# Small products wait for company before they enter the stream of projections

## The chip, the cores and the metric

The kernel runs on one core of one Trainium2 chip. The metric is the device time of one execution in microseconds (us). Three executions took 1216.67, 1216.26 and 1215.63 us (median 1216.26); the execution that was profiled took 1215.75 us.

## The reference

Three transformer-like layers are applied to 256 tokens of width 1024, all in fp32. Layers 0 and 1 have the same form (`hybrid_layer`): a projection `h @ w_in` makes the inputs of three branches, a native sparse attention (NSA, 8 heads of 64), a gated linear attention (GLA, 4 heads) and a cross-attention into 256 memory tokens (4 heads of 128). Their outputs are multiplied with branch weights, gated and summed, projected by `w_out`, added to x, and then an MLP of width 4096 with a squared ReLU follows. Layer 2 (`hybrid_layer_2`) has a spatial gating branch, a depthwise convolution of 31 taps with a layer norm, and an attention of 8 heads of 64 (MoBA), merged in the same way. Cut to the frame:

```python
x = first_block(x, mem, ...)      # DEPTH = 2 times hybrid_layer
return second_block(x, ...)       # once hybrid_layer_2
# hybrid_layer: z = rms_norm(x) @ w_in; o_nsa, o_gla, o_mem from parts of z
merged = gates0 * (o_nsa @ w_branch[0]) + gates1 * (o_gla @ w_branch[1]) + gates2 * (o_mem @ w_branch[2])
x = x + merged @ w_out
return x + jnp.square(jax.nn.relu(rms_norm(x) @ w_up)) @ w_down
```

## The kernel before

Every large fp32 product is made of three fp32r products: activations and weights are each split into a rounded high part and the rest (`hi` and `lo`, tiles `hx`, `oh`, `ol`, `b8x`). Weights come in units of 128 x 1024 by DMA (`raw`); ScalarE or GpSimd makes `hi` (L441, L439), VectorE makes `lo` (L442). These large products write the four PSUM banks `acc` and are called the stream here. 512-column products of the stream follow one another every 0.227 us, 256-column ones every 0.12 us.

Everything else on TensorE is small: transposes against the identity (L192), attention scores, the GLA levels, the sums over heads. These are written as Python generators, called chains. A chain emits a few products and the work on the other engines that depends on them, then yields a number: how many nanoseconds later, by the order's own clock, its next step shall come. The small products use three PSUM banks `psm` and one, `pso`, for sums over several steps.

The order of TensorE's instructions is written out by hand, in the order in which Python emits them (`manual_schedule` for PE alone, L119 and around); the other engines' orders are found by the framework. The order's clock is a number that each emitted product advances by an estimate (`pe_time` L175: 217.6 for a 512-column fp32r product, 108.8 for a 256-column one, n x 1.69 but at least 214 for an fp32 product, 107 for a transpose). The rules:

- `start` (L143) puts a chain on the list `chains` with a due time. `advance` (L130) runs one step of it and sets the next due time to the clock plus the yielded number; an ended chain leaves the list.
- `pump` (L138) is called from inside the stream and advances every chain that is due. `tok_major` (L493) calls it after three 512-column products, `transposed` (L507) after six 256-column ones: every 652.8 of the clock either way. `up_first` (L1365) calls it after two products, `dn` after three.
- `finish(c)` (L148) advances chains in the order of their due times, moving the clock ahead where needed, until `c` has ended. `need(hh, k)` (L157) does the same until the part k of a transposed activation has been emitted.

The chains that matter here. In layers 0 and 1: `mem_chain` (L639), `nsa_qk` (L699), `nsa_cmp` (L758), `nsa_att` (L882) and `gla` (L991) are alive together while the projections of gates and values stream. `nsa_att` yields 350 again and again until q and k are there and the memory attention has ended. The stream calls `finish` for the memory chain, `gla` and `nsa_att` (L1302 to L1308) before the branch product that reads each. At a layer's end `x_transposed` (L539) transposes the new x in four steps of four transposes: for the last two it yields 2750 until `halves` says that the second half of x is there, then 1000 (`XLAT`), then a step, 300, and the last step. Its result `hx` is needed by `up_first`, whose second half begins with part 4. In layer 0 alone a further chain, the transposition of the memory for layer 1, is started 7000 ahead of its first step before `up_first` (L1402).

In layer 2: `conv` (L1468) has 30 steps of VectorE work with 5000 between them, then a product with ones for the mean (four products of 256 columns), 4450 later one for the variance, and then the norm. `moba` (L1521) is started 1000 ahead, when 48 pumps have passed since `conv` began. It has twelve steps with products: scores (1729 of the clock), 6500 later the next scores, 6500 later transposes (642), 2000 later the sums (1298), 3000 later scores, and so on. 80 pumps later the stream reaches `finish(c_att)` (L1617), after 16 products `psm<-a,n` without a pump. From there the stream has 128 pumps (gates and branch product of branches 2 and 0, gates of branch 1) to `finish(c_conv)` (L1632), behind which the norm's result is split into `oh`, `ol` and multiplied with the branch weights. When `moba` has ended, `conv` is the only chain on the list.

Of the kernel before, what the change touches and what calls it, by code (L numbers as in the profile page):

```python
# [29 lines left out]
WARM2 = 4  # L30
NRAW = 4
XLAT = 1000.0
CO_IDENT = 0
CO_HM = 128
CO_CM = CO_HM + 8
# [11 lines left out]
def shape_constants():  # L47
    p = np.arange(128)
    cf = np.zeros((128, CO_END), np.float32)
    cf[:, CO_IDENT:CO_IDENT + 128] = np.eye(128)  # L50
    ml = np.zeros((9, 128, 128), np.float32)
# [47 lines left out]
def block_kernel(ctx, tc, x_in, mem_in, positions, ln_mix, w_in, b_merge, nsa_q_norm, nsa_k_norm,  # L99
# [27 lines left out]
    clock = [0.0]  # L127
    chains = []

    def advance(c):  # L130
        lat = next(c[0], None)
        if lat is None:
            c[2] = True
            chains.remove(c)
        else:
            c[1] = clock[0] + LATF * lat

    def pump():  # L138
        for c in list(chains):
            while not c[2] and c[1] <= clock[0]:  # L140
                advance(c)
# [94 lines left out]
    def PS():  # L236
        return psm.tile([P, 512], F32, tag="psm", name=nm("psm"))
# [59 lines left out]

    IDF = CF[:, CO_IDENT:CO_IDENT + 128]
    IDB = CBT[:, CB_IDENT:CB_IDENT + 128]
# [193 lines left out]
    def tok_major(hh, hl, w2d, r0, nk, cols, fine=False, paired=None):  # L493
        n = sum(c1 - c0 for c0, c1 in cols)
        ps = [ACC(), ACC()]
        ws = units(w2d, r0, nk, cols, paired, fine)
        for k, (wh, wl) in enumerate(ws):
            need(hh, k)
            if fine and k == 0:
                warm(WARM2)  # L500
            for tt in range(2):
                ts_ = slice(tt * P, tt * P + P)
                mm3(ps[tt][:, :n], hh[:, k, ts_], hl[:, k, ts_], wh, wl, k == 0, k == nk - 1)
                pump()
        return ps

    def transposed(hh, hl, w2d, r0, nk, c0, ps, paired=None):  # L507
        ws = units(w2d, r0, nk, [(c0, c0 + 256)], paired)
        for cb in range(2):
            o = ps[:, cb * 256:cb * 256 + 256]  # L510
            for k, (wh, wl) in enumerate(ws):
                cs = slice(cb * P, cb * P + P)
                mm(o, wh[:, cs], hh[:, k, :], k == 0, False)
                mm(o, wh[:, cs], hl[:, k, :], False, False)
                mm(o, wl[:, cs], hh[:, k, :], False, k == nk - 1)
                if k % 2 == 1:
                    pump()
        return ps
# [20 lines left out]
    def x_transposed(src, hh, hl, gcol, prog, halves):  # L539
        for k in range(0, 8, 2):  # L540
            if halves is not None:
                if halves[0] <= k // 4:
                    while halves[0] <= k // 4:
                        yield 2750.0
                    yield XLAT
            pt = PS()
# [665 lines left out]
    def layer(l, hT):  # L1212
# [116 lines left out]
        def up(gi):  # L1329
            uh, ul = OT()  # L1330
            p2 = up_first() if gi == 0 else None
            for c in range(2):
                r = T2("gtmp")
                ws = units(w_up[l], 0, 8, [(gi * 512 + c * 256, gi * 512 + c * 256 + 256)]) if gi else None
                for cb in range(2):
                    rs = r[:, 256 * cb:256 * cb + 256]
                    if gi == 0:
                        ps = p2[2 * c + cb]
                    else:
                        ps = PS()  # L1340
                        for part in range(2):
                            for k in range(8):
                                up_product(ps, k, cb, ws[k][part], part)
                            pump()
                    act(rs, ps[:, 256:512], AF.Copy)
                    dve.tensor_tensor(rs, ps[:, 0:256], rs, op=OP.add)
                act(r, r, AF.Relu)  # L1347
                uhf = uh[:, 2 * c:2 * c + 2].rearrange("p a b -> p (a b)")
                ulf = ul[:, 2 * c:2 * c + 2].rearrange("p a b -> p (a b)")
                act(uhf, r, AF.Square)  # L1350
                u = T2("tmp")
                pool.tensor_tensor(u, r, r, op=OP.mult)  # L1352
                dve.tensor_tensor(ulf, u, f32(uhf), op=OP.subtract)
            ub[gi] = (uh, ul)
# [365 lines left out]
```

## Time and profile before

| what | value |
|---|---|
| median of three executions | 1216.26 us |
| profiled execution, and its span | 1215.75 us, 1214.0 us |
| TensorE products (PE) | 1195.1 us busy, 98% of the span, 6553 instructions |
| VectorE (DVE), ScalarE (ACT), GpSimd (POOL) | 72%, 50%, 17% busy |
| HBM read | 211.86 MB, 175 GB/s over the span |

The span is the time between the first and the last instruction. PE rows are products, DVE, ACT and POOL rows are those engines; a row gives its start in us from the span's start, its length, the engine, the line of the code, what it writes and reads, the shape and how many like it follow directly. An [idle before <- what] at the end tells how long the engine had been idle and what it waited for. Products are pipelined and their ends are modelled, so the distance from start to start tells more than a length.

### The profile page before, as it was taken

Reading aid. Unit: us, or ns where it says so; the run is one execution under the profiler, and the core shown is the slowest. Engines: PE = TensorE matmul, PEld = TensorE weight load, DVE = VectorE, ACT = ScalarE, POOL = GpSimd, SP = SyncE. Lnnn points to the kernel's source line nnn. Section 1 sums busy time; section 2 is a strip of 40 time slices with the busy share of each in tenths; the row PEclk is TensorE's granted clock in tenths of the full one; section 3 lists DMA queues with packets and bytes.
Section 4 is the critical chain, followed back from the end, with each engine's and each line's share of the span. In section 5 each row is a group of like instructions: output and inputs, shape, how many; then the busy total and the mean of one; then the engine's idle time right before and its main releaser. Section 6 shows DMA issues by size and latency. Waiting matters only on the chain. (4 is left out here: it accounts for less than half of the span.)

```text
span 1214.0 us, 17754 instructions
## 1 busy us (share of the span) xinstructions
PE 1195.1 (98%) x6553; PEld 1001.3 (82%) x6553; DVE 869.8 (72%) x1457; ACT 605.0 (50%) x988; POOL 202.1 (17%) x235
## 2 busy tenths in 40 slices
PE   8999999999999999999999999999999999999997
PEld 6897777888888888888777888888888998998886
DVE  5967878667755556658878867665555699995587
ACT  7567544434645545466645444464454344453351
POOL 2310320120111112200222020121121111010201
PEclk9999999999999999999999999999999999999999
DMA  8567533677566666657723576656566655557652
GB/s 278 182 179 198 156 97 112 191 214 214 166 188 189 192 191 190 181 157 187 199 65 105 176 197 195 187 175 196 185 192 198 195 170 162 153 158 212 186 195 87
DMA packets 138699, 213.91 MB, mean 176 GB/s; under 512 B 12145, under 2 KB 76757, under 8 KB 138612
## 3 DMA queue, kind: packets, MB, share of 16 engines
q1 hardware_dynamic: 137284, 209.19, 57.9%
q0 software_dynamic: 1152, 3.31, 0.9%
q8 instruction: 51, 0.84, 0.3%
q14 instruction: 36, 0.29, 0.1%
q10 hardware_dynamic: 176, 0.27, 0.1%
HBM read 211.86 MB, written 1.05 MB: 175 GB/s over the span
## 5 line engine op out<-in xcount | busy, mean ns | idle before, releaser
L442 DVE TENSOR_TENSOR lo<-raw,hi 128x1024 fp32r<-128x1024 f32 (+1 forms) x369 | 458.1, 1245 | 218.5 <-ACT hi L441 163.0
L441 ACT ACTIVATE hi<-raw 128x1024 fp32r<-128x1024 f32 (+1 forms) x308 | 322.6, 1057 | 331.2 <-PE acc L188 267.5
L188 PE MATMUL acc<-hi,hx 128*128 128x512 f32 (+1 forms) x1024 | 337.6, 394 | 0.0
L188 PEld LDWEIGHTS acc<-hi,hx 128*128 128x128 f32 x1024 | 191.3, 188 | 40.0 <-issue 4.0
L188 PE MATMUL acc<-lo,hx 128*128 128x512 f32 (+1 forms) x512 | 196.9, 385 | 0.1
L439 POOL TENSOR_SCALAR hi<-raw 128x1024 fp32r<-128x1024 f32 x61 | 75.5, 1238 | 601.3 <-PE acc L188 424.4
L188 PE MATMUL acc<-hi,oh 128*128 128x512 f32 x400 | 157.9, 395 | 0.0
L188 PE MATMUL acc<-hi,ol 128*128 128x512 f32 x400 | 155.9, 390 | 0.0
L188 PE MATMUL acc<-lo,oh 128*128 128x512 f32 x400 | 155.9, 390 | 0.0
L188 PE MATMUL acc<-hx,hi 128*128 128x256 f32 (+1 forms) x704 | 136.6, 297 | 0.9 <-DVE hx L532 0.7
L188 PEld LDWEIGHTS acc<-hx,hi 128*128 128x128 f32 x704 | 111.0, 191 | 6.0 <-issue 2.3
L188 PE MATMUL psm<-hx,hi 128*128 128x512 f32 x448 | 111.8, 391 | 0.0
L188 PEld LDWEIGHTS acc<-lo,hx 128*128 128x128 f32 x512 | 96.5, 189 | 16.7 <-DVE lo L442 0.6
L188 PE MATMUL acc<-hi,b8x 128*128 128x512 f32 (+1 forms) x336 | 105.0, 385 | 0.0
L188 PE MATMUL acc<-hx,lo 128*128 128x256 f32 x384 | 99.7, 283 | 0.0
L188 PEld LDWEIGHTS psm<-hx,hi 128*128 128x128 f32 x448 | 81.4, 189 | 15.1
L188 PEld LDWEIGHTS acc<-hi,ol 128*128 128x128 f32 x400 | 75.1, 188 | 16.2 <-DVE ol L532 0.3
L188 PEld LDWEIGHTS acc<-hi,oh 128*128 128x128 f32 x400 | 75.2, 188 | 14.6
L188 PEld LDWEIGHTS acc<-lo,oh 128*128 128x128 f32 x400 | 75.2, 188 | 14.5
L188 PEld LDWEIGHTS acc<-hi,b8x 128*128 128x128 f32 x336 | 62.2, 188 | 11.7 <-ACT b8x L531 0.2
L188 PEld LDWEIGHTS acc<-hx,lo 128*128 128x128 f32 x384 | 69.9, 191 | 0.6
L1352 POOL TENSOR_TENSOR tmp<-gtmp 128x512 f32<-128x512 f32 x32 | 40.1, 1253 | 166.9 <-ACT gtmp L1347 166.9
(359 smaller groups left out, 1456.9 us busy)
## 6 DMA issues: line engine op xcount, KB each, us to landing
raw<-in_w_in SPq DMA_DIRECT2D x160, 512.0 KB
raw<-in_w_up SPq DMA_DIRECT2D x64, 512.0 KB
raw<-in_w_down SPq DMA_DIRECT2D x64, 512.0 KB
raw<-in_w_branch SPq DMA_DIRECT2D x28, 512.0 KB
raw<-in_w_out SPq DMA_DIRECT2D x24, 512.0 KB
raw<-in_cmp_w SPq DMA_DIRECT2D x32, 256.0 KB
raw<-in_mem_w_kv SPq DMA_DIRECT2D x15, 512.0 KB
raw<-in_w_branch SPq DMA_DIRECT2D x16, 256.0 KB
```

What stands on the lines that cost most here:

```text
L188: nc.tensor.matmul(o, l, r, start=start, stop=stop, skip_group_check=True)
L439: pool.tensor_scalar(hi, raw, 1.0, 1.0, op0=OP.mult, op1=OP.mult)
L441: act(hi, raw, AF.Copy)
L442: dve.tensor_tensor(lo, raw, f32(hi), op=OP.subtract)
L1352: pool.tensor_tensor(u, r, r, op=OP.mult)
```

## The change

`pump` first collects the chains that are due. If there is exactly one, more than one chain is on the list, and the one is less than 800 late on the order's clock, nothing is advanced at this pump. Otherwise all due chains are advanced as before. `finish` and `need` are unchanged.

```diff
+COMPANY = 800
     def pump():
+        due = [c for c in chains if c[1] <= clock[0]]
+        if len(due) == 1 and len(chains) > 1 and clock[0] - due[0][1] < COMPANY:
+            return
         for c in list(chains):
             while not c[2] and c[1] <= clock[0]:
                 advance(c)
```

## Rows read from the trace of the kernel before

**Rows 1.** The page: busy time of each engine, and the chain that ended last by engine.
```profile
PE 1195.1 (98%) x6553; PEld 1001.3 (82%) x6553; DVE 869.8 (72%) x1457; ACT 605.0 (50%) x988; POOL 202.1 (17%) x235
...
PE 33%; DVE 1%; ACT 1%; POOL 0%; issue 0%; DVEq 0%; POOLq 0%; ACTq 0%
```

**Rows 2.** Busy time by stretch (us, then PE, PEld, DVE, ACT, POOL with their counts, granted clock, DMA share, GB/s): the chains of layer 0 after the polling, the stretch behind it, and the chains of layer 1.
```profile
114.00:212.00 98.00, 95.35 (x574) 73.33 (x573) 82.75 (x203) 53.27 (x128) 20.38 (x29) 1.00 0.42 125
212.00:300.00 88.00, 88.00 (x405) 73.01 (x404) 60.39 (x64) 37.43 (x44) 13.50 (x11) 1.00 0.70 205
...
582.00:684.00 102.00, 98.51 (x584) 75.69 (x583) 85.42 (x205) 53.76 (x129) 22.08 (x29) 0.98 0.42 123
```

**Rows 3.** Timeline of PE in these stretches: the longest waits of small products.
```profile
140.11 0.68 PE L188 MATMUL psm<-QB,b8x 128*128 128x128 f32 x4 [0.76 <-DVE tmp L798]
...
149.44 0.55 PE L192 MATMUL psm<-CF,pexp 128*128 128x128 f32 x3 [0.86 <-DVE a L1061]
...
620.69 0.21 PE L192 MATMUL psm<-CF,ck 32*128 32x32 f32 x1 [0.83 <-DVE ck L834]
...
647.39 0.68 PE L188 MATMUL psm<-QB,b8x 128*128 128x128 f32 x4 [1.26 <-DVE a L1061]
```

**Rows 4.** Busy time by stretch in layer 1, right behind 32 products of 16 columns; the column after POOL is the granted clock.
```profile
628.00:631.00 3.00, 3.00 (x14) 1.56 (x13) 2.59 (x12) 0.90 (x2) 0.00 (x0) 0.64 0.00 0
631.00:634.00 3.00, 3.00 (x12) 2.41 (x11) 1.32 (x6) 1.55 (x2) 1.01 (x2) 0.80 0.00 0
```

**Rows 5.** Timeline of PE: four transposes alone in the stream (the product before them, they, and the second product after them).
```profile
273.52 0.39 PE L188 MATMUL acc<-hi,ol 128*128 128x512 f32 x1
273.75 0.60 PE L192 MATMUL psm<-CF,M 128*128 128x128 f32 x4
...
274.42 0.40 PE L188 MATMUL acc<-lo,oh 128*128 128x512 f32 x1
```

**Rows 6.** Timeline of PE, the stream's last product before an entry and its second after it: eight products of `nsa_cmp` alone; a step of `nsa_att` with these eight and four of `gla`; the same step with `gla` alone.
```profile
125.33 0.39 PE L188 MATMUL acc<-hi,hx 128*128 128x512 f32 x1
...
126.56 0.39 PE L188 MATMUL acc<-lo,hx 128*128 128x512 f32 x1
...
130.91 0.40 PE L188 MATMUL acc<-hi,hx 128*128 128x512 f32 x1
...
134.92 0.39 PE L188 MATMUL acc<-lo,hx 128*128 128x512 f32 x1
...
182.04 0.40 PE L188 MATMUL acc<-hi,hx 128*128 128x512 f32 x1
...
185.29 0.39 PE L188 MATMUL acc<-lo,hx 128*128 128x512 f32 x1
```

**Rows 7.** Timeline of PE in layer 0: the last transposes of `gla`, and the first product that reads its result.
```profile
211.64 1.04 PE L192 MATMUL psm<-CF,g 128*128 128x128 f32 x8
...
232.95 0.39 PE L188 MATMUL acc<-hi,oh 128*128 128x512 f32 x1
```

**Rows 8.** Timeline of PE in layer 0, `up_first`: products of the first half's second column block, the last two steps of `x_transposed` (`psm<-CF,X`), the second half's first products, its last part.
```profile
303.80 1.09 PE L188 MATMUL acc<-hx,hi 128*128 128x512 f32 x4
304.73 0.60 PE L192 MATMUL psm<-CF,X 128*128 128x128 f32 x4
...
305.62 0.60 PE L192 MATMUL psm<-CF,X 128*128 128x128 f32 x4
...
307.47 1.56 PE L188 MATMUL acc<-hx,hi 128*128 128x512 f32 x6
...
309.59 0.74 PE L188 MATMUL acc<-hx,hi 128*128 128x512 f32 x2
```

**Rows 9.** Timeline of DVE at the same place (the low parts of `hx`, parts 4, then 5 and 6), and of PE at the like place of layer 1.
```profile
305.87 0.48 DVE L532 SCALAR_TENSOR_TENSOR hx<-psm,COL,hx 128x256 fp32r<-128x256 f32 x1 [0.46 <-ACT hx L531]
306.77 0.88 DVE L532 SCALAR_TENSOR_TENSOR hx<-psm,COL,hx 128x256 fp32r<-128x256 f32 x2 [0.41 <-ACT hx L531]
...
780.40 0.73 PE L188 MATMUL acc<-hx,hi 128*128 128x512 f32 x2 [0.74 <-DVE hx L532]
```

**Rows 10.** Timeline of PE in layer 2: scores of `moba` (first and second), its last transposes, and the 16 products ahead of `finish(c_att)`.
```profile
1011.73 0.93 PE L188 MATMUL psm<-g,g 64*128 64x128 f32 x8
...
1019.85 0.93 PE L188 MATMUL psm<-g,g 64*128 64x128 f32 x8
...
1072.98 0.82 PE L192 MATMUL psm<-CF,pexp 128*128 128x128 f32 x6
...
1078.92 1.95 PE L188 MATMUL psm<-a,n 128*128 128x128 f32 x16
```

**Rows 11.** Timeline of ACT: the two copies that follow the transposes at 1072.98.
```profile
1073.57 0.88 ACT L1556 ACTIVATE pts<-psm 128x384 f32<-128x384 f32 x2 [0.89 <-PE psm L192]
```

**Rows 12.** Timeline of PE: the products of `conv` for the mean and for the variance, and the third product of the branch that reads its result.
```profile
1144.00 1.89 PE L188 MATMUL psm<-b8x,cw 128*128 128x256 f32 x8
...
1150.52 1.89 PE L188 MATMUL psm<-b8x,cw 128*128 128x256 f32 x8
...
1172.23 0.50 PE L188 MATMUL acc<-hi,ol 128*128 128x512 f32 x1
```

**Rows 13.** Timeline of DVE: the first instruction of the norm, and the low part of the branch input at its end.
```profile
1153.78 0.42 DVE L1487 TENSOR_SCALAR a<-psm 128x256 f32<-128x256 f32 x1
...
1170.96 1.21 DVE L532 SCALAR_TENSOR_TENSOR ol<-b8x,oh 128x1024 fp32r<-128x1024 f32 x1
```

## The prediction, made before the change was run

> **What bounds the kernel now.** I read the page first: TensorE (PE) is busy 98% of the span, and the chain that ended last is PE too, the other engines having 1% each or less [rows 1]. So the time is the sum of PE's products plus the places where PE waits, and a change of the order pays or costs only there. Next the busy times by stretch: PE idles 98.00 - 95.35 = 2.65 us while the chains of layer 0 run, 102.00 - 98.51 = 3.49 us in layer 1, and nothing in the 88 us behind them [rows 2]. Together 6.1 us. The timeline of PE shows who waits: small products that come before their input (made by VectorE or GpSimd) or their bank is free, 0.76, 0.86, 0.83 and 1.26 us for the longest [rows 3]. Behind one long run of tiny products in layer 1 the granted clock is 0.64 and 0.80 over two stretches of 3 us [rows 4]: PE fell to 1.2 GHz for 3 x 0.36/0.5 + 3 x 0.20/0.5 = 3.4 us, which is 1.7 us of lost work. Last I read the places where the stream waits for a chain: the end of a layer [rows 8, 9] and layer 2 [rows 10 to 13].
>
> **Part 1: what an entry costs.** From the last stream product before four transposes to the second after them is 274.42 - 273.52 = 0.90 us; two distances of the stream are 0.45, so the four cost 0.45, and 4 x 0.109 (the distance inside a longer run) is 0.44 [rows 5]. An entry by itself costs some 0.01 us. Eight products of the compression alone cost 126.56 - 125.33 - 0.45 = 0.78 us. The three chains together cost 134.92 - 130.91 - 0.45 = 3.56, the same without these eight 185.29 - 182.04 - 0.45 = 2.80 [rows 6]: in company they cost 0.76. Joining saves 0.01 to 0.02 us. I counted 37 entries in the timeline of each of layers 0 and 1 from 114 us (583 us) on; if a third of the 74 joins, that is 25 x 0.015 = 0.4 us. Bounds 0 and -0.4; I take **-0.1**, since the joins mix kinds.
>
> The Trainium skill (TensorEngine Tiling (Array Packing), Key Properties) says that a change of tiling mode, not of tile, drains TensorE. By that rule each avoided entry could save two drains. The eight narrow products above do show a small step (0.78 us alone), but in company they still change mode against their neighbours, and only 0.02 us goes; the trace bears out a small cost of the mode and none that joining removes. What it would give if it did is among the rivals.
>
> **Part 2: the chains in layers 0 and 1.** A pump comes every 652.8 of the order's clock, 3 x 0.227 = 0.68 us. A lone step is held to the next pump, or to the one after it if it was found less than 147 late. Until about 114 us `nsa_att` polls every 350, so it is due at every pump and gives company to all: nothing is held there. Afterwards a step of 800 (`gla`'s levels) comes after three pumps where it came after two. `gla` has about 41 pumps of hold from there if always alone, 41 x 0.68 = 28 us, some 18 with company a third of the time. Its last transposes stand at 211.64, and the product that needs them at 232.95 [rows 7]: 21 us of room. `nsa_att` is needed a branch later still. So the delay costs nothing at `finish`; at the extreme 7 us too late. What changes is the waits: the same work of VectorE, 82.75 us in 98 [rows 2], is spread over some 18 us more, and lone products come 0.68 us later to their input. Where steps now come in pairs, two softmaxes and masked copies ask for VectorE at once and three `psm` banks serve both. Bounds: all 6.1 us and the clock's 1.7 go (-7.8), or the waits double (+6.1). I take half the waits gone, clock as it was: **-3.1**: of the four long waits two (620.69, 647.39) are of the first product of an entry, which a hold only brings later to its input, and two of products behind others in the same entry, which it doesn't help [rows 3].
>
> **Part 3: x at the end of layer 0.** With the memory's chain on the list, all three last steps of `x_transposed` are alone and held. By the code's numbers from the start of `up_first`: the poll, due at 13398, is resumed at 14347 (before: 13477); +1000, due 15347, is held until 16306, after the third pair of low products of the second column block; the last step is due at 17034 and held at 17386 and, 788 late, at 17822; then `need` forces it straight before part 6. Before, it stood at 305.62 [rows 8]. In time: the block's eight high products take 303.80 to 305.62 without the two insertions, three low pairs to 306.34; there the transposes stand (before: 304.73). Part 4 of `hx` was ready 305.87 + 0.48 - 304.73 = 1.62 us after the transposes' start, part 5 2.5 us after [rows 8, 9]. So part 4 comes at 307.96 and PE, there at 307.02, waits 0.94; part 5 at 308.84, 0.43 more. The last transposes start at 309.29; part 6 is ready at 310.91 (1.18 idle), part 7 at 311.8 after the memory's first transposes. Before, part 7 started at 309.59 behind the same transposes [rows 8]: **+2.1**. If a 1.23 us weight split gets between, 3.4; if DVE is quicker with one part at a time, 1.0. In layer 1 the chain is alone on the list; its stall of 0.74 [rows 9] stays.
>
> **Part 4: layer 2, `moba`.** I counted the order's clock from `moba`'s start, 80 pumps. Before, `moba` acts at pumps 2, 12, 22, 26, 31, 41, 45, 50, 60, 64, 74, 78; check: 10 pumps x 0.68 + 1.3 own = 8.1 us, and the trace has 1019.85 - 1011.73 [rows 10]. With the hold, and company where `conv` is due too, it acts at 2, 14, 24, 29, 35, 45, 50, 56, 66, 71; the last transposes and sums are left for `finish(c_att)`. There nothing streams between them: the copies start 0.59 us after the transposes' start and take 0.88 [rows 11], the transposes 0.66, so PE idles about 0.6 before and between the sums. **+0.6**; 2.2 if ACT has a 1.06 us weight split in the way, 0.4 at least.
>
> **Part 5: layer 2, `conv`.** Its taps are long computed, but its steps are held too: 2, 9, 16, 24, 30, 37, 45, 51, 58, 66, 72 and held at 80, against 1, 7, 13, 21, 27, 33, 41, 46, 52, 60, 65, 73, 79 before. `finish(c_att)` moves the clock by the 2000 and 1000 of `moba`'s end while no stream passes, which gives some back: step 20 comes at pump 9 behind it, where it came at pump 5. Alone afterwards, `conv` is 4 pumps late to its end: 2.7 us on the products at 1144.00 and 1150.52 [rows 12]. From there to `ol` (1170.96 + 1.21 = 1172.17 [rows 13]) everything was just in time: the product that reads it starts at 1172.23 [rows 12]. Of the 18.4 us from 1153.78 to 1172.17 weight splits took some 3 in between, on DVE and ACT; those are due at the stream's time, not the norm's, and 2.7 us later most are past. I take **+0.8** of the 2.7; bounds 0 and 2.7.
>
> **The sum.** -0.1 - 3.1 + 2.1 + 0.6 + 0.8 = +0.3 us on the profiled 1215.75 (span 1214.0 and 1.75 around it), which is 0.5 below the median of the runs: 1216.26 + 0.3 = **1216.6**.
>
> **The rivals.**
> *The hold cures the waits.* All 6.1 us and part of the slow clock go (-7) with parts 3 to 5 as above (+3.5): 1212.7. For: lone GLA products wait up to 1.26 us for the masked copy before [rows 3]. Against: VectorE stays 84% busy there [rows 2]. 0.20.
> *A drain per entry.* If every one of 25 avoided entries saved 0.2 us: 1216.6 - 5 = 1211.6. Against: rows 5 and 6. 0.04. It is the skill's rule above, taken at its word.
> *Pairs collide (slower).* GLA levels behind another chain's scores wait more often, since pairs are now sought: the 6.1 us of waits grow by half instead of halving, +3.1 for -3.1: 1222.8. For: the 0.76 us wait stands right behind `nsa_att`'s scores. It decides as soon as the waits of the two stretches stay above 5.1 us, for 5.1 - 6.1 - 0.1 + 3.5 is +2.4. 0.22.
> *Late chains cost their upper bounds (slower).* Parts 3 to 5 at 3.4 + 2.2 + 2.7 = 8.3 in place of 3.5: 1221.4. 0.12.
> *It doesn't do what it says.* So much company that hardly a step moves: 1216.3. Against: the counts of parts 4 and 5. 0.04.
>
> **Chances.** A measurement of this kernel tells 0.2%, 2.4 us, from no change. The forecast has 0.38, its own range 1213.8 to 1218.7. Faster 0.20 + 0.04 = 0.24; same 0.38 + 0.04 = 0.42; slower 0.22 + 0.12 = 0.34. For 8 in 10 the range takes in most of both sides: 1211.5 to 1222.5.
>
> **What would show it.** Part 1: four lone transposes still cost 0.45 us. Part 2: GLA's last transposes 10 to 25 us later, PE idle in the two stretches near 3 us in place of 6.1. Part 3: PE waits for `hx` from DVE near 307 to 311 us in layer 0, three times, and not more in layer 1. Part 4: transposes and sums of `moba` directly behind the 16 products `psm<-a,n`, with a wait for `pts` between. Part 5: the mean's product 4 pumps later behind these, and a wait for `oh` or `ol` ahead of the last branch product. The forecast is wrong if the idle time of the two stretches grows, or if PE waits more than 3 us in one of parts 3 to 5.

## The result, and the profile after

The changed kernel takes 1231.31 us (median of 4 runs, 1228.33 to 1233.91), beside 1216.47 for the kernel before on the same chip: ratio 1.0118 with an interval of 1.0104 to 1.0131. The profiled execution took 1229.73 us, 13.98 more than the 1215.75 of before. The rows below name lines that are 4 higher than in the rows of before.

The page of the changed kernel: busy time of each engine, and the chain that ended last by engine, as in [rows 1].
```profile
PE 1202.0 (98%) x6553; PEld 1006.8 (82%) x6553; DVE 871.3 (71%) x1457; ACT 605.9 (49%) x988; POOL 195.4 (16%) x235
...
PE 29%; DVE 5%; issue 1%; ACT 1%; POOL 0%; DVEq 0%; ACTq 0%
```
The instructions are the same in number. PE is busy 6.9 us longer with the same products, most of it a matter of its clock (the table below has 5.1), and the chain that ended last now runs through VectorE for 5% of the span, where it was 1%.

To see where the time went I laid the two timelines of PE side by side. The stream has the same 5224 products in the same order in both, so the start of a product can be compared with the start of the same product before; what the difference gains over a stretch is that stretch's loss. All of it is in six places (us, profiled executions):

| stretch of the kernel before | change | of it waits of PE | of it PE's clock |
|---|---|---|---|
| layer 0, chains (94 to 219) | +2.5 | -0.2 | +3.4 |
| layer 0, `up_first` (304 to 310) | +3.7 | +3.2 | 0 |
| layer 1, chains (588 to 690) | -2.2 | -1.7 | 0 |
| layer 2, behind `moba`'s second scores (1031 to 1078) | +6.2 | +4.5 | +1.7 |
| layer 2, at `finish(c_att)` (1079) | +0.9 | +0.2 | 0 |
| layer 2, branch product of `conv` (1172) | +3.0 | +3.0 | 0 |

The table is that of one execution. The mean granted clock of the four executions was 0.988 to 0.994; that of 57 executions of the kernel before, run beside the experiments, was 0.992 to 0.998 with a median of 0.996. Taken as lost work, (1 - clock) times the span, that is an estimate of 11 us after and 5 before at the median, so by medians some 6 of the 14.8 us are the clock's.

Timeline of PE after, the waits of small products in the two chain stretches, as in [rows 3].
```profile
151.35 0.21 PE L196 MATMUL psm<-CF,ck 32*128 32x32 f32 x1 [1.41 <-DVE ck L838]
...
179.99 0.68 PE L192 MATMUL psm<-QB,b8x 128*128 128x128 f32 x4 [1.03 <-DVE a L1065]
...
625.57 0.21 PE L196 MATMUL psm<-CF,ck 32*128 32x32 f32 x1 [1.41 <-DVE ck L838]
...
651.94 0.68 PE L192 MATMUL psm<-QB,b8x 128*128 128x128 f32 x4 [0.34 <-DVE a L1065]
```
Four waits of 4.2 us in all are left, where [rows 2] had 6.1. But the wait for the compressed key `ck`, 0.83 us in layer 1 before, is now 1.41 in both layers.

Busy time by stretch after (us; PE, PEld, DVE, ACT, POOL with their counts; then the granted clock, DMA share, GB/s): the chains of layer 0, and then those of layer 1, the 4 us of the 32 scores against the compressed key (16 columns each) in layer 0, and the 7 us behind them.
```profile
114.00:219.00 105.00, 102.55 (x594) 79.76 (x593) 85.08 (x204) 55.23 (x130) 19.25 (x30) 0.97 0.43 129
588.00:690.00 102.00, 100.22 (x590) 77.85 (x590) 86.98 (x203) 53.32 (x128) 21.21 (x30) 0.98 0.45 134
...
156.00:160.00 4.00, 4.00 (x39) 3.95 (x37) 1.19 (x2) 1.67 (x9) 0.00 (x0) 1.00 0.38 131
160.00:167.00 7.00, 7.00 (x24) 4.88 (x25) 3.83 (x14) 1.61 (x3) 0.00 (x0) 0.51 0.00 1
```
PE waits 2.45 and 1.78 us in these stretches. From 160.06 on it runs at 1.2 GHz for 6.83 us, though it was busy without a wait in the 8 us before: a loss of 3.4 us that the kernel before did not have in layer 0 [rows 2]. In layer 1 the fall of [rows 4] is there again, 3.41 us at 634.51.

Timeline of PE after in layer 0's `up_first`, as in [rows 8], and of DVE beside it.
```profile
308.89 0.60 PE L196 MATMUL psm<-CF,X 128*128 128x128 f32 x4
...
311.49 0.73 PE L192 MATMUL acc<-hx,hi 128*128 128x512 f32 x2 [1.77 <-DVE hx L536]
312.52 0.73 PE L192 MATMUL acc<-hx,hi 128*128 128x512 f32 x2 [0.30 <-DVE hx L536]
313.09 0.60 PE L196 MATMUL psm<-CF,X 128*128 128x128 f32 x4
314.77 0.73 PE L192 MATMUL acc<-hx,hi 128*128 128x512 f32 x2 [1.08 <-DVE hx L536]
```
```profile
309.82 1.23 DVE L446 TENSOR_TENSOR lo<-raw,hi 128x1024 fp32r<-128x1024 f32 x1 [1.87 <-PE acc L192]
310.96 0.48 DVE L536 SCALAR_TENSOR_TENSOR hx<-psm,COL,hx 128x256 fp32r<-128x256 f32 x1
```
The last steps of `x_transposed` come late, PE waits three times, and a weight split of 1.23 us stands before part 4 of `hx`.

Timeline of PE after in layer 2: `moba`'s second scores, the product that waits longest, then the end of `moba` [rows 10], the products of `conv` and the branch that reads them [rows 12].
```profile
1025.14 0.93 PE L192 MATMUL psm<-g,g 64*128 64x128 f32 x8
...
1040.47 0.40 PE L192 MATMUL acc<-hx,lo 128*128 128x256 f32 x1 [4.51 <-DVE lo L446]
...
1087.46 1.95 PE L192 MATMUL psm<-a,n 128*128 128x128 f32 x16
1089.24 0.97 PE L196 MATMUL psm<-CF,pexp 128*128 128x128 f32 x6
1090.38 1.34 PE L192 MATMUL pso<-pts,n 128*64 128x256 f32 x8 [0.16 <-ACT pts L1560]
...
1157.74 1.89 PE L192 MATMUL psm<-b8x,cw 128*128 128x256 f32 x8
...
1183.95 0.50 PE L192 MATMUL acc<-hi,oh 128*128 128x512 f32 x1 [1.45 <-ACT oh L535]
...
1186.21 0.50 PE L192 MATMUL acc<-hi,ol 128*128 128x512 f32 x1 [1.52 <-DVE ol L536]
```
The largest single loss is a product of the stream, not a small one: 4.51 us for the low part `lo` of a weight.

Timeline of DVE after, ahead of that product: the gating branch's layer norm (L1598 to L1600), then the split; and in the second fence the same place before.
```profile
1035.35 1.53 DVE L1598 TENSOR_SCALAR n<-acc,bmv,brs 128x512 f32<-128x512 f32 x2 [0.64 <-POOL brs L1597]
1036.79 1.28 DVE L1599 TENSOR_TENSOR n<-n,a 128x512 f32<-128x512 f32 x2
1037.99 1.28 DVE L1600 TENSOR_TENSOR n<-n,a 128x512 f32<-128x512 f32 x2
1039.20 2.35 DVE L446 TENSOR_TENSOR lo<-raw,hi 128x1024 fp32r<-128x1024 f32 x2
```
```profile
1030.61 0.81 DVE L1594 TENSOR_SCALAR n<-acc,bmv,brs 128x512 f32<-128x512 f32 x1
...
1031.43 1.19 DVE L442 TENSOR_TENSOR lo<-raw,hi 128x1024 fp32r<-128x1024 f32 x1
...
1035.61 1.22 DVE L442 TENSOR_TENSOR lo<-raw,hi 128x1024 fp32r<-128x1024 f32 x1
1036.74 0.69 DVE L1596 TENSOR_TENSOR n<-n,a 128x512 f32<-128x512 f32 x1
```
Before, the splits stand among the norm's instructions; after, all six of the norm come first. The order of VectorE is found by the framework when the kernel is built, and it came out otherwise because `moba`'s second scores stand two pumps later in PE's order (1025.14, before 1019.85 [rows 10]; 3.9 of these 5.3 us had been lost ahead of it). That it is this step which turns the order, two experiments below show. The Trainium skill (PSUM — Partial Sum Buffer, Engine vs sequencer instructions) calls VectorE's queue strictly first in, first out; the rows agree: the split at 1039.20 runs behind the norm, which itself had waited 0.64 us for GpSimd.

### The profile page after: what moved, and what is told of

It reads as the page before. It is cut to its first block, busy times and chain, and to the rows that moved or that the text cites. A ratio compares the mean times of both kernels' runs of the same rounds, so it can differ in the third digit from the quotient of the medians.

```text
span 1228.0 us, 17743 instructions
## 1 busy us (share of the span) xinstructions
PE 1202.0 (98%) x6553; PEld 1006.8 (82%) x6553; DVE 871.3 (71%) x1457; ACT 605.9 (49%) x988; POOL 195.4 (16%) x235
## 5 line engine op out<-in xcount | busy, mean ns | idle before, releaser
L443 POOL TENSOR_SCALAR hi<-raw 128x1024 fp32r<-128x1024 f32 x61 | 72.8, 1193 | 628.6 <-PE acc L192 435.4
```

The source lines that it names most:

```text
L443: pool.tensor_scalar(hi, raw, 1.0, 1.0, op0=OP.mult, op1=OP.mult)
```

## The experiments

My theory after reading: the loss is made of separate places, each a chain's step held past its input's use (x in layer 0, the second scores, `conv`); the hold among the chains of layers 0 and 1 pays nothing. The rival was a common cause, the waits for company as such or PE's clock. The first three runs split the change by place, with a flag around the new test.

**Hold only among the chains of layers 0 and 1.**
```diff
-        if len(due) == 1 and len(chains) > 1 and clock[0] - due[0][1] < COMPANY:
+        if hold[0] and len(due) == 1 and len(chains) > 1 and clock[0] - due[0][1] < COMPANY:
...
+        hold[0] = True
         w = w_in[l]
...
         mem1 = []
+        hold[0] = False
         hh, hl, hc = out_proj(w_out[l], mg, fin, 16 + 8 * l,
```


> The hold acts only in layers 0 and 1 from the layer's first projection to its output projection. Theory (the loss sits in three places behind these chains): the same as before within 2.5 us, 1214 to 1219, GLA's transposes some 8 us later, PE's idle time in the two stretches no larger than 6.1 us; what moves is where the clock falls. Rival (every held step costs, by waits or by a slower clock): two thirds of all held steps are here, so two thirds of the loss, 1224 or more.

1217.29 us (before 1217.19), ratio 0.9996 [0.9984, 1.0009]. No change, as expected: fewer waits, but the clock was at 1.2 GHz for 6.83 us in each layer of the profiled run (at 158.74 and 629.78).

**Hold only from the output projection to the end of `up(0)`.** The same flag, set there.

> The hold acts only from the output projection of a layer to the end of its first MLP step. Theory: +3.7 us, 1220, with PE waiting about 1.8, 0.3 and 1.1 us for hx in layer 0 and nothing new in layer 1. Rival (the delay is hidden by other work): under +1 us.

1221.23 us, ratio 1.0040 [1.0026, 1.0053]. The three waits are there with 1.77, 0.29 and 1.08 us, the like products lose 3.66 us across them, and layer 1 lost nothing.

**Hold only in layer 2.** The same flag.

> The hold acts only in layer 2. Theory: +10 us, 1226.5: a wait of some 4.5 us for a weight split at the second scores, and 3 us ahead of the last branch product. Rival (these waits come from the shifted order of layers 0 and 1, by the way the framework then orders VectorE): under +5 us, with one of the two waits missing.

1226.72 us, ratio 1.0080 [1.0065, 1.0095]. Waits of 4.53, 1.45 and 1.52 us; the like products lose 10.7 us in layer 2 of the profiled run. The three parts add up: by their medians +0.1, +4.0 and +9.5, together 13.6, beside 14.8 for the whole change.

**The second scores two pumps later, without any hold.** In the kernel before, one number.
```diff
-                    yield 6500.0 if pr == 0 else 3000.0
+                    yield 7805.6 if pr == 0 else 3000.0
```


> The kernel before, without any hold, but moba's second scores come two pumps later (its first yield is 7805.6 in place of 6500). Theory (the place of the second scores against the layer norm of the gating branch decides): a wait of 3 to 5 us for the low part of a weight, +4 to +7 us, 1220 to 1223. Rival (the wait needs the whole changed order, conv's steps too): no wait over 1 us there, 1216 to 1217.5.

1227.73 us, ratio 1.0092 [1.0077, 1.0107]: more than expected. PE timeline of this kernel, the wait:
```profile
1036.72 0.58 PE L188 MATMUL acc<-hx,lo 128*128 128x256 f32 x1 [4.51 <-DVE lo L442]
```
So the wait comes from the place of these eight products alone, not from the hold. The rest came from elsewhere: the clock fell behind the wait (6.83 us at 1.2 GHz), and `conv` ended three pumps later, with 1.24 and 1.53 us of waits at its branch and a second fall.

**The second scores one pump later.** 7152.8 in place of 7805.6.

> The kernel before, moba's second scores one pump later (7152.8 in place of 6500), not two. The framework then keeps weight splits between the layer norm's VectorE instructions, as before. Theory (the order on VectorE decides, not the delay): no wait over 1 us at the second scores; conv's last products come one pump later, so up to 0.7 us; 1217 to 1218.5. Rival (the delay of the scores decides in proportion): half of the wait, 2.2 us, and half of the loss, 1221.

1220.25 us, ratio 1.0027 [1.0014, 1.0040]. PE timeline, the place of the long wait:
```profile
1034.33 0.39 PE L188 MATMUL acc<-hx,lo 128*128 128x256 f32 x1 [0.63 <-DVE lo L442]
```
It is 0.63 us here; VectorE's order has the splits among the norm as before. So one pump more or less decides between two orders. But the time is above what I expected: `conv` is one pump late, its branch waits 0.90 and 1.52 us, and the clock fell there (6.83 us at 1176.52).

**The norm shortened.** As with two pumps, with the norm's gain and bias left out: four of its six VectorE instructions.
```diff
-            dve.tensor_tensor(VN[tt], VN[tt], VG[0], op=OP.mult)
-            dve.tensor_tensor(VN[tt], VN[tt], VG[1], op=OP.add)
```


> The kernel of the second scores two pumps late, with the gain and the bias of the gating branch's layer norm left out (four VectorE instructions of 0.6 us; the output changes). Theory (the splits wait behind the norm's block on VectorE): the block is 2.4 us shorter, so PE's wait of 4.5 us becomes 2.1. Rival (the wait is for ScalarE, whose high parts stand behind the exponentials of the scores): the wait stays at 4 us or more.

1227.65 us (1222.85 in the profiled run), ratio 1.0090 [1.0070, 1.0110]. Timelines of PE and, below, of DVE:
```profile
1034.60 0.39 PE L188 MATMUL acc<-hx,lo 128*128 128x256 f32 x1 [2.12 <-DVE lo L442]
```
```profile
1031.88 1.53 DVE L1594 TENSOR_SCALAR n<-acc,bmv,brs 128x512 f32<-128x512 f32 x2 [0.64 <-POOL brs L1593]
1033.33 1.22 DVE L442 TENSOR_TENSOR lo<-raw,hi 128x1024 fp32r<-128x1024 f32 x1
```
The wait shrinks by 2.39 us, the four instructions took 2.41 (1036.79 to 1039.20 after). That the norm in front of the split makes the wait is shown by this trace; the median, 1227.65 beside 1227.73 with the whole norm, does not show it. The three executions without a profile had a granted clock of 0.989 to 0.991, the profiled one 0.996; where they lost the clock is not on record.

**`conv` four pumps later, without any hold.**
```diff
-                yield 5000.0
+                yield 5000.0 + (2611.2 if t == 30 else 0.0)
```


> The kernel before, but conv's last yield of 5000 is 2611.2 longer, so that its products for mean and variance come four pumps later, as in the changed kernel, and nothing else moves. Theory (the end of conv has no room): PE waits ahead of the last branch product, 2.5 to 3.5 us together, 1220. Rival (the norm's chain has room once the weight splits are past, my 0.8 us of the prediction): a wait under 1.2 us, 1217 to 1218.

1222.85 us, ratio 1.0045 [1.0028, 1.0062]. PE timeline:
```profile
1175.36 0.50 PE L188 MATMUL acc<-hi,oh 128*128 128x512 f32 x1 [1.46 <-ACT oh L531]
...
1177.61 0.80 PE L188 MATMUL acc<-hi,ol 128*128 128x512 f32 x1 [1.52 <-DVE ol L532]
1178.20 0.63 PE L188 MATMUL acc<-hi,oh 128*128 128x512 f32 x1
```
The waits are those of the change. The last row shows what I had not expected: 512-column products that take 0.43 us from one to the next, not 0.227, for the clock fell at 1176.84 for 6.83 us.

**`conv` two pumps later.** 1305.6 in place of 2611.2.

> The kernel before, with conv's end alone put two pumps later. Between the experiment with one pump (waits of 0.90 and 1.52 us for the branch input's two parts, 1220.25) and the one with four (1.46 and 1.52, 1222.85). Theory (a step: the parts' last instructions fall behind two weight splits as soon as they are a pump late, and a further pump adds little): two waits of together 2.4 to 3.0 us, and the clock at 1.2 GHz right behind them, 1220 to 1223. Rival (linear, a pump lost is a pump waited for): 1.35 us of waits, half of those at four pumps, and a time of about 1218.5.

1221.28 us, ratio 1.0033 [1.0022, 1.0045]; one wait of 2.36 us, and 1.2 GHz for 3.41 us behind it. The tail costs 2.4 us at one pump, 2.4 at two, 3.0 at four: a step, not a slope.

**The change with three exemptions**: no hold from the output projection to the end of `up(0)`, none for `conv`, none for `moba` ahead of its second scores.
```diff
+        if (hold[0] and len(due) == 1 and len(chains) > 1 and due[0][0] not in free_now
+                and clock[0] - due[0][1] < COMPANY):
...
```


> The changed kernel with the hold lifted in three places: the steps of x_transposed at the end of a layer, moba's second scores, and conv's steps. Theory (these three places are the whole loss): none of the waits of 1.8, 4.5 and 1.5 us, conv's products five pumps earlier than in the kernel before, and the same time within 2 us, 1215.5 to 1219.5. Rival (the hold costs beyond these places, by a slower clock): 1221 or more.

1218.91 us, ratio 1.0012 [0.9999, 1.0026]: 1.8 us above the kernel before where the whole change is 14.8 above it. The waits named above for x and `conv` are gone, and of the 4.51 us at the second scores 0.41 is left. What remains are mainly the two waits for `ck` and 6.83 us at 1.2 GHz at the 32 scores in each layer.

**The compressed key two pumps later, on top of the exemptions.**
```diff
-        yield 3900.0
+        yield 5205.6
```


> The change with its three exemptions (1218.91), and in layers 0 and 1 the transposition of the compressed key comes two pumps later, so that PE need not wait for it (1.41 us twice). Theory: these two waits go and 2.8 us with them, 1215.5 to 1217; the clock still falls to 1.2 GHz behind the 32 products of 16 columns in both layers, for a long run of narrow products stands in front of it either way. Rival: the waits some microseconds ahead of these products are what the clock falls for; then the two periods at 1.2 GHz go as well (2 x 3.4 us): 1210 to 1213.

1216.57 us, ratio 0.9989 [0.9978, 1.0000]. The waits for `ck` are gone. Busy time by stretch in layer 1, the 32 scores and the 4 us behind them:
```profile
621.00:625.00 4.00, 4.00 (x38) 3.91 (x37) 1.25 (x2) 1.99 (x9) 0.00 (x0) 1.00 0.50 133
625.00:629.00 4.00, 4.00 (x19) 2.66 (x18) 2.98 (x13) 0.90 (x2) 0.00 (x0) 0.57 0.00 0
```
PE did not wait in layer 1's stretch ahead of them, and the clock still fell there, so it does not need the waits; in layer 0 it did not fall in this run.

**The 32 scores in two entries of 16, on top of that.**
```diff
         for tt in range(2):
+            if tt:
+                yield 300.0
             for h in range(8):
```


> As the one with the later compressed key, and the 32 products of 16 columns are split in two entries of 16, a pump apart. Theory: what the clock falls for is the long run of narrow products (GLA's level, 32 scores, four of 2 columns: 5 to 6 us on end), so at half its length it stays at 2.4 GHz: no period at 1.2 GHz near 160 and 630 us, 1210 to 1213. Rival: the clock falls there in any case, or for the waits: the same time as the one before it within 1 us, 1.2 GHz still there.

1212.52 us (1211.79 to 1213.29), ratio 0.9958 [0.9945, 0.9970]: 0.4% faster than the kernel before. Timeline of PE in layer 1, and busy time by stretch around it and at the same place in layer 0:
```profile
622.98 1.86 PE L196 MATMUL psm<-KB,b8x 128*128 128x16 f32 x16
...
626.82 1.96 PE L196 MATMUL psm<-KB,b8x 128*128 128x16 f32 x16
```
```profile
622.00:629.00 7.00, 7.00 (x57) 6.05 (x56) 1.78 (x5) 2.59 (x10) 0.00 (x0) 1.00 0.23 78
156.00:163.00 7.00, 7.00 (x53) 5.96 (x52) 2.22 (x10) 2.70 (x10) 0.00 (x0) 1.00 0.24 74
```
The clock stays at 2.4 GHz in both layers. One cost of the hold is still in it: the like products lose 2.0 us while `moba` runs, 1.4 of them at `finish(c_att)`.

**These two edits in the kernel before, without any hold.**

> The kernel before, without any hold, with the two edits of the preceding kernel: compressed key two pumps later, 32 scores split in two entries. Theory: its wait of 0.83 us for the key at 620.69 and the 3.4 us at 1.2 GHz behind 628 go (1.7 us): 1214.0 to 1215.5, faster than the kernel before by 2 to 3. Rival: the rest of the chain, up to two pumps and a half later, runs into a wait elsewhere: 1217 or more.

1221.60 us, ratio 1.0033 [1.0019, 1.0046]: the rival came true. The clock no longer falls behind 628, but `nsa_att` ends later and meets the end of `gla`. Timeline of PE, then of DVE:
```profile
213.19 0.98 PE L192 MATMUL psm<-CF,g 128*128 128x128 f32 x7 [1.89 <-DVE g L1105]
```
```profile
210.39 1.22 DVE L442 TENSOR_TENSOR lo<-raw,hi 128x1024 fp32r<-128x1024 f32 x1
...
211.72 0.69 DVE L1104 TENSOR_TENSOR a<-a,g4ry 128x512 f32<-128x512 f32 x1
212.45 0.69 DVE L1105 TENSOR_TENSOR g<-a,g 128x512 f32<-128x512 f32 x1
```
GLA's last norm stands behind a weight split and comes 1.89 us late, and the clock falls at 214.63. The like products lose 4.9 us in layer 0. In layer 1 the same wait of 1.89 us comes at 686.08, and 0.7 us is lost. So the gain of the preceding version is not that of its two small edits by themselves: with the exempted hold they gave some 6 us (1.8 above the kernel before to 4.4 below it), without it they cost 4.7. Which part of the hold's order spares GLA's end there was not tried alone.

## Why the prediction was wrong

I predicted 1216.6 us, +0.3 on the profiled time; it was 1231.31, +14.0 profiled. Of the signs that I had named, PE waited 3.15 us in part 3 and 4.51 in the stretch of part 4, both over the 3.

**No step covered the largest term.** Part 4 put `moba`'s second scores at pump 14 in place of 12, which is where they went, and priced only its end. I had no term for what the two pumps do to VectorE's order. That cost +6.2: 4.51 of wait and 1.7 of clock. The scores one pump and two pumps later, and the shortened norm, show it.

**Part 1** expected a third of 74 entries to join. Counted in the timeline, the stream of the whole kernel is interrupted 175 times before and 169 times after; the hold delays much and joins little. Its price was near nothing either way. The rule of the Trainium skill on drains (TensorEngine Tiling (Array Packing), Key Properties) was not put to a test; no run here shows it.

**Part 2** foresaw half the waits gone, -3.1, with the clock as it was. The waits fell by 1.9 (6.14 to 4.23 us), as the first products of an entry did not all gain: `ck` waits 1.41 us twice. And the clock was not as it was: +3.4 in layer 0, where the profile of before, with no fall, had been a lucky one (last section). Together the two stretches gave +0.3 and not -3.2; some 1.2 us of gain in them is neither waits nor clock, and stays unexplained. The hold among these chains alone moved nothing by the median (1217.29 beside 1217.19). GLA's last transposes came at 219.62, 8 us later than [rows 7], a little under the 10 I had named as least.

**Part 3** had the mechanism right step by step: the transposes behind the third low pair, part 6 forced by `need`, three waits for `hx`, none new in layer 1. The size was off: 3.7, not 2.1. The weight split that I gave only to the upper bound (3.4) is there at 309.82.

**Part 4**, the end of `moba`: transposes and sums directly behind the 16 products, +0.9 for the +0.6 expected.

**Part 5** had `conv` 4 pumps late, which the stream's count shows exactly. The step that failed is that most of the weight splits between the norm and the branch would be past by then, so that 0.8 of the 2.7 remained. Timeline of DVE after, as in [rows 13]: the norm's first instruction, the splits behind it and the low part; and in the second fence the splits of that stretch before.
```profile
1166.74 0.42 DVE L1491 TENSOR_SCALAR a<-psm 128x256 f32<-128x256 f32 x1
...
1170.50 1.22 DVE L446 TENSOR_TENSOR lo<-raw,hi 128x1024 fp32r<-128x1024 f32 x1
...
1174.15 1.22 DVE L446 TENSOR_TENSOR lo<-raw,hi 128x1024 fp32r<-128x1024 f32 x1
...
1179.55 1.22 DVE L446 TENSOR_TENSOR lo<-raw,hi 128x1024 fp32r<-128x1024 f32 x1
...
1182.67 2.35 DVE L446 TENSOR_TENSOR lo<-raw,hi 128x1024 fp32r<-128x1024 f32 x2
1184.94 1.21 DVE L536 SCALAR_TENSOR_TENSOR ol<-b8x,oh 128x1024 fp32r<-128x1024 f32 x1
```
```profile
1157.53 1.22 DVE L442 TENSOR_TENSOR lo<-raw,hi 128x1024 fp32r<-128x1024 f32 x1
...
1161.17 1.22 DVE L442 TENSOR_TENSOR lo<-raw,hi 128x1024 fp32r<-128x1024 f32 x1
...
1167.84 3.19 DVE L442 TENSOR_TENSOR lo<-raw,hi 128x1024 fp32r<-128x1024 f32 x2
```
The norm's first instruction came 1.9 us late (1166.74 for 1153.78, with 11.0 us lost ahead of it), so 0.8 of the 2.7 was regained by then. But behind it five splits of some 1.2 us stand where four stood (one of them, at 1174.15 after and 1161.17 before, runs while the norm waits for ScalarE anyway). So the low part came 2.95 us late, and PE waited 2.97 us, a little over the upper bound. The order of VectorE is fixed; a late chain does not find it emptier.

The rival of late chains at their upper bounds was the nearest in kind: two of its three bounds were reached and passed (3.7 for 3.4, 3.0 for 2.7). It summed to 1221.4 because the sum kept the -3.1 of part 2 and knew neither the new order nor the clock.

## What to carry to other kernels

Where one engine's order is written by hand and the others' are derived from it, moving a few small products by a pump can turn the order of a busy engine; price a moved step by rebuilding that order and reading what then stands ahead of the weight preparation, not by the step's own delay. A policy that delays steps should leave out those whose result the stream needs next, and a chain that ends just in time should be taken to have no room at all. Where PE's clock falls at a dense run of narrow products, try dividing the run among wide ones: here that gave 4.1 us (1216.57 to 1212.52) on the exempted hold, though the same cut in the order without a hold, together with the later key, came out slower.

## What the runs showed of the hardware that I had not expected

The granted clock fell to 1.2 GHz while PE was busy without a wait (4.00 of 4.00 us at 156 to 160 after). In the 12 profiled kernels that had the 32 scores of 16 columns in one run, it fell at them in 18 of 24 places, for 3.41 or 6.83 us: in five while they ran, in the others within 1.1 us of the start of the last one. In the 2 kernels with two runs of 16 it fell in none of 4. What it is in these products that does it is not shown. Seven experiments left the order of layer 0's chains as it was before, and in six of them it fell there, so the 1.00 of [rows 2] was one execution's luck. It also shows in the spread: 24 runs of the kernel before took 1215.11 to 1221.66 us beside the last experiments, with a granted clock of 0.993 to 0.998; five of the version with split scores took 1211.79 to 1213.29, with 0.998 to 0.999. The Trainium skill (TensorE: Matmul & The Clock Gate, Part 1: The HAM clock gate) says that the clock is set by how busy PE has been of late; a PE that the profile calls fully busy, but with products of 16 columns, lost it here.

Behind waits it fell too, by one profiled execution each: in all three kernels with the 4.5 us wait in layer 2, in none with 0.63 or 2.12 us there, and at the branch of `conv`, with 2.4 to 3.0 us of waits, in five of seven.
